# Half of a modulation's later columns computed by TensorE products instead of VectorE sums

## The chip, the core and the metric

The kernel runs on one core of one Trainium2 chip. Its engines are TensorE (PE in the rows, its weight loads PEld), VectorE (DVE), ScalarE (ACT), GpSimd (POOL) and SyncE (SP, which issues the transfers). The metric is the device time of one launch in microseconds, as the median of several runs.

## The reference, cut to what matters

Two transformer blocks of two layers each run one after the other over 512 tokens of width 1024; the first block also carries a context of 256 tokens. Each layer of the first block is steered by six vectors (shift, scale and gate, once for attention and once for the feed-forward part), which come from the condition vectors `c` and `c_ctx`:

```python
silu_c = jax.nn.silu(c)
silu_cc = jax.nn.silu(c_ctx)
for l in range(DEPTH):
    mod = silu_c @ w_ada[l] + b_ada[l]
    sh_a, sc_a, g_a, sh_f, sc_f, g_f = jnp.split(mod[:, None, :], 6, axis=-1)
    mc = jnp.split(silu_cc @ w_ada[l][:, :n_c] + b_ada[l][:n_c], n_c // d)
    hx = rmsnorm(x) * (1 + sc_a) + sh_a
    ...
    x = x + g_a * (jnp.concatenate([fx, ax, rx], axis=-1) @ w_out[l])
    x = x + g_f * swiglu(rmsnorm(x) * (1 + sc_f) + sh_f, w_gate[l], w_up[l], w_down[l])
```

So `mod` is a product of two vectors (1024 values each) with a matrix of 1024 x 6144, in single precision.

## The kernel before

Activations lie with the feature on the partition, so a vector of 1024 values is eight columns of 128. The six steering vectors of a layer are 48 columns; `mod[l][:, q, j]` is column j for the tokens (q = 0) or for the context (q = 1). Column j needs the 128 x 1024 slice `w_ada[l, j]`, one transfer of 512 KB. Columns 0 to 15 of layer 0 (shift and scale of the attention part) are made in an opening stage, `opening`, before anything else can run. Columns 16 to 39 of layer 0 are made by the generator `mod_cols` during the first mixing stage (attention, a gated recurrence called hgrn, and a Fourier mix), columns 40 to 47 and those of layer 1 during the first feed-forward stage. In the mixing stage all of them go the same way: for each of the two condition vectors one VectorE instruction (L524) multiplies the 128 x 1024 slice with the silu vector, which `sic[q]` holds on all partitions, and sums each row into one value of `mod`. In the opening some columns go another way, marked `"P"`: eight TensorE products (L1662) take a 128 x 128 block of the slice, stored in transposed order, as weights and the two silu vectors (`csil`, 128 x 2) as the moving side, and so make both values of the column in a bank of PSUM at once.

Matrix products of the layers are done in three rounds of rounded halves (`mm3`, L246 to L248): high times high, high times low, low times high. Each weight tile of 128 x 1024 is loaded, rounded by ScalarE (L231), and its rest taken by VectorE or GpSimd (L233).

The mixing stage `Mix1.rest` weaves generators: `dense` (all projections of the normed input), `hgrn(0)` and `hgrn(1)`, `fourier`, `attention` (which starts when `dense` is done) and `mod_cols`; `_weave` takes the next step of the one with the least time spent by numbers written in the code (`MCOST`, 4 units per column and vector). That fixes the program's order; a scheduler with a timing model of its own then places the instructions of each engine. Buffers come from an arena that hands out the slot which has been free the longest, and PSUM is eight banks handed out in the same way. Each engine runs its queue in order. SyncE's queue is also in order: a transfer into a slot that is not free yet holds up all transfers behind it.

Lines that the prediction's steps touch: L519 (issue of `w_ada`), L524 (the product and sum), L526 and L527 (the same on GpSimd and ScalarE, used in layer 1), L538 (adds `b_ada`), L1662 (the opening's TensorE columns), L757 (a product with a 128 x 2 moving side in `heads`), L893 and L898 (hgrn's products and their merge), L871 (the first step of an hgrn), L912 (its decay factors), L614 (transposes), L1007 (split of the queries), L588, L592 and L593 (softmax: maximum, scaling of it, exponential), L1036 (transposes of its result).

Of the kernel before, what the change touches and what calls it, by code (L numbers as in the profile page):

```python
# [12 lines left out]
AF = mybir.ActivationFunctionType  # L13
# [4 lines left out]
KD = 8  # L18
# [45 lines left out]
class _Arena:  # L64
# [32 lines left out]
    def fr(self, *bufs):  # L97
        for b in bufs:
            if isinstance(b, (list, tuple)):
                self.fr(*b)  # L100
                continue
            h = b.home
            assert (h.freed[b.o:b.o + b.u] == np.inf).all()
            h.clock += 1
            h.freed[b.o:b.o + b.u] = h.clock
# [28 lines left out]
def scaled(g, f):  # L134
    for c in g:
        yield c and c * f
# [7 lines left out]
def _body(tc, xc, cvec, w_ada, w_in, w_four, w_out, gu, dn, cols, ab_in, ab_out, gates, c_in, c_out,  # L144
          k_id, k_hs, k_lm, k_cm, k_dft, k_dftc, k_bd, k_rope, xsc, out, stop=None, dbg=None, mark=lambda n: None):
    nc = tc.nc
    V, A, G, PE, SP = nc.vector, nc.scalar, nc.gpsimd, nc.tensor, nc.sync
# [9 lines left out]
    with es:  # L157
# [8 lines left out]
        mod = [per.tile([128, 2, 48], F32, name=f"mod{i}") for i in range(2)]  # L166
        hpost = per.tile([128, 48], F32, name="hpost")
        csil = per.tile([128, 16], F32, name="csil")
# [15 lines left out]
        al, alr, fr = arena.al, rarena.al, arena.fr  # L184
# [17 lines left out]
        pf_ = banks.fr  # L202
# [311 lines left out]
        def mod_cols(l, jobs, which, sic):  # L514

            for j0, n, plus1 in jobs:
                for j in range(j0, j0 + n):
                    r = al(1024)
                    (G if MODQ else SP).dma_start(r.f, w_ada[l, j])  # L519
                    for q in which:  # L520
                        t = r if q == which[-1] else al(1024)
                        acc = mod[l][:, q, j:j + 1]
                        if j % 4 in MODV[l]:
                            V.scalar_tensor_tensor(t.f, r.f, 1.0, sic[q].f, op0=ALU.mult, op1=ALU.mult, accum_out=acc)  # L524
                        else:
                            G.tensor_tensor(t.f, r.f, sic[q].f, ALU.mult)  # L526
                            A.activation(t.f, t.f, AF.Copy, accum_out=acc)  # L527
                        if t is not r:
                            fr(t)
                    fr(r)  # L530
                    yield MCOST * len(which)
                mod_fin(l, j0, n, plus1, which)
# [84 lines left out]
        class Mix1(Phase):  # L617
# [491 lines left out]
            def rest(self, nxt):  # L1109
# [6 lines left out]
                mods = () if last else (mod_cols(0, MODS, (0, 1), self.sic),)  # L1116
                c = PACE[l]
                h0, h1, fo, at = (scaled(g, c[i]) for i, g in ((1, self.hgrn(0)), (1, self.hgrn(1)), (3, self.fourier()), (2, self.attention())))
# [659 lines left out]
OPEN = ('P', 'VV', 'P', 'P', 'P', 'VV', 'P', 'VV', 'P', 'VV', 'P', 'P', 'P', 'VV', 'P', 'VV')  # L1778
# [9 lines left out]
PRE = (3, 0, 2, 2, 3)  # L1788
ONPOOL = ('dg1', 'dh001', 'dh002', 'dh003', 'dh004', 'dh005', 'dh006', 'dh007', 'dh101', 'dh102', 'dh103', 'dh104', 'dh105', 'dh106', 'dh107', 'ka005', 'ka011', 'ka012', 'ka013', 'ka014', 'ka015', 'ka016', 'ka017', 'ka112', 'ka113', 'ka114', 'ka115', 'ka116', 'ka117', 'kk00', 'kl1', 'ma0', 'og10', 'qa001', 'qa002', 'qa003', 'qa004', 'qa005', 'qa006', 'qa007', 'qa011', 'qa012', 'qa013', 'qa015', 'qa016', 'qa101', 'qa102', 'qa103', 'qa104', 'qa105', 'qa106', 'qa107', 'qa111', 'qa112', 'qa116', 'qa117', 'qm00', 'qm11', 'r11', 'r20', 'r21', 'zd1')
MODQ = 0  # L1790
PACE = ((1.2, 1, 1, 1, 0), (1, 1.2, 0.85, 1, 0), (1, 1.5, 1))
MODV = ((0, 1, 2, 3), (2,))
ADAV = ((2, 4, 6), (0, 2, 4, 5), (0, 2, 4, 6))
POSTG = ((0, 1, 2, 3, 4, 5, 6, 7),) * 5 + ((0, 2, 4),)
MCOST = 4.0
# [10 lines left out]
def _feat(v):  # L1806

    v = np.asarray(v)
    return v.reshape(-1, 128).T
# [61 lines left out]
def _pack(inp):  # L1871
    a = {k: np.asarray(v) for k, v in inp.items()}
    r = _constants()
    xc = np.concatenate([a["ctx"][0], a["x"][0]], 0)
    r["xc"] = np.ascontiguousarray(xc.T.reshape(KD, 128, W).transpose(1, 0, 2))
    r["cvec"] = np.stack([a["c"][0], a["c_ctx"]])
    r["w_ada"] = np.ascontiguousarray(a["w_ada"].transpose(0, 2, 1).reshape(2, 48, 128, D))
    for j in range(2 * KD):
        if OPEN[j] == "P":
            r["w_ada"][0, j] = _blk(a["w_ada"][0][:, j * 128:j * 128 + 128], KD, 1).reshape(128, D)  # L1880
    r["w_in"] = np.stack([_blk(a["w_in"][l], KD, 18) for l in range(2)])
    r["w_four"] = np.ascontiguousarray(a["w_four"].reshape(2, 2, 128, 256).transpose(0, 2, 1, 3))
    r["w_out"] = np.stack([_blk(a["w_out"][l], KD, KD) for l in range(2)])
    fs = [("w_gate", "w_up", "w_down", l) for l in range(2)]
    for l in range(2):
        fs += [(f"ffn{i}_w_gate_2", f"ffn{i}_w_up_2", f"ffn{i}_w_down_2", l) for i in (1, 2)]
    r["gu"] = np.stack([np.stack([_blk(a[n][l], KD, NF) for n in (g, u)], 2) for g, u, _, l in fs])
    r["dn"] = np.stack([_blk(a[d][l], NF, KD) for _, _, d, l in fs])
    r["ab_in"] = _blk(a["ab_w_in_2"][0], KD, 20)
    r["ab_out"] = _blk(a["ab_w_out_2"][0], KD, KD)  # L1890
    ci = _blk(a["c_w_in_2"][0], KD, 24).reshape(3, KD, 128, KD, 128)
    r["c_in"] = np.ascontiguousarray(ci[[1, 2, 0]].transpose(1, 0, 2, 3, 4))
    r["c_out"] = _blk(a["c_w_out_2"][0], KD, KD)
    g = np.zeros((128, 4, 256), np.float32)
    for i, n in enumerate(("lru_gate_a_w_2", "lru_gate_x_w_2")):
        for h in range(8):
            o = h % 2 * 64
            g[o:o + 64, h // 2, i * 128 + o:i * 128 + o + 64] = a[n][0, h]
    r["gates"] = g
    two = lambda v: np.concatenate([v, v])  # L1900
    cols = np.zeros((128, NCOL), np.float32)
    vals = {
        "b_ada0": _feat(a["b_ada"][0]), "b_ada1": _feat(a["b_ada"][1]),
        "cc": _feat(r["cvec"]), "lb": _feat(a["hg_lb_logits"]), "fin": _feat(a["final_norm"]),
        "pre": _feat(a["norm_pre_2"]), "post": _feat(a["norm_post_2"]),
        "lconv": a["lru_conv_w_2"][0].reshape(4, 4, 128).transpose(2, 1, 0).reshape(128, 16),
        "lconvb": _feat(a["lru_conv_b_2"]), "lba": _feat(a["lru_gate_a_b_2"]), "lbx": _feat(a["lru_gate_x_b_2"]),
        "llam": _feat(a["lru_lambda_2"]),
        "cconv": a["c_conv_w_2"][0].reshape(3, KD, 128).transpose(2, 1, 0).reshape(128, 24),
    }  # L1910
    for l in range(2):
        vals[f"qn{l}"] = two(a["q_norm"][l])[:, None]
        vals[f"kn{l}"] = two(a["k_norm"][l])[:, None]
        vals[f"hn{l}"] = two(a["hg_norm"][l])[:, None]
    for n, (o, w) in _COLS.items():
        cols[:, o:o + w] = vals[n]
    r["cols"] = cols
    return {n: np.ascontiguousarray(r[n]) for n in _INS}
# [17 lines left out]
```

## Time and profile before

| | |
|---|---|
| median of 3 runs | 3787.3 us |
| lowest, highest | 3782.1, 3798.88 us |
| the profiled execution | 3782.26 us |
| its span | 3780.3 us |
| PE busy | 3631.1 us (96%), 19768 instructions |
| PEld busy | 3121.2 us (83%) |
| DVE busy | 1903.9 us (50%) |
| ACT busy | 1425.1 us (38%) |
| POOL busy | 557.7 us (15%) |
| mean granted clock of PE | 0.983 |

The span is the time from the first to the last instruction; 1.96 us of the execution lie outside it. Busy time of PE is modelled: products are pipelined, so that a busy PE need not be at its peak. The profile's PEclk is the granted clock: 1.00 is 2.4 GHz and 0.50 is 1.2 GHz. The stages that matter here: the opening up to about 58 us, the projections (`dense`) with hgrn(0) up to about 257 us, attention with hgrn(1) and Fourier up to about 480 us, then the output projection and the feed-forward stage.

### The profile page before, as it was taken

What the parts mean: (1) busy time and instruction counts of PE and PEld (TensorE: products, weight loads), DVE (VectorE), ACT (ScalarE), POOL (GpSimd) and SP (SyncE); (2) the same over time, 40 slices, a digit from 0 to 9 for tenths busy, and PEclk for the clock granted to TensorE, in tenths of its full rate; (3) what the DMA queues carried; (4) which work ended last, traced back from release to release, by engine and by line L of the source; (5) the groups of instructions that cost most, each with busy time, mean ns of one, the idle gap of its engine ahead of it and who ended that gap; (6) DMA issues with size and microseconds to landing.
All of it is one profiled execution on the core that took longest, in us unless ns stands there. A gap on an engine that the chain in (4) does not pass through costs nothing. (4 is left out here: it accounts for less than half of the span.)

```text
span 3780.3 us, 48445 instructions
## 1 busy us (share of the span) xinstructions
PE 3631.1 (96%) x19768; PEld 3121.2 (83%) x19768; DVE 1903.9 (50%) x2833; ACT 1425.1 (38%) x2410; POOL 557.7 (15%) x499
## 2 busy tenths in 40 slices
PE   7998899999999989999999999999999999999998
PEld 7876698888887869888988886788888888888887
DVE  6677655533344775333533367562345234645234
ACT  4235643342243474323432335442234233334222
POOL 1331012550013400000100031110011001111001
PEclk9998999999999999999999999999999999999999
DMA  6322114453212122423132221133222322223322
GB/s 210 93 73 85 44 44 137 150 188 99 76 40 71 40 80 76 134 73 110 59 106 89 93 77 62 51 109 104 86 82 96 106 86 88 91 89 104 107 71 76
DMA packets 95823, 345.12 MB, mean 91 GB/s; under 512 B 10864, under 2 KB 14064, under 8 KB 95600
## 3 DMA queue, kind: packets, MB, share of 16 engines
q1 hardware_dynamic: 95024, 341.50, 28.0%
q8 instruction: 155, 2.54, 0.3%
q14 instruction: 68, 0.56, 0.0%
q10 hardware_dynamic: 576, 0.52, 0.0%
HBM read 334.64 MB, written 4.19 MB: 90 GB/s over the span
## 5 line engine op out<-in xcount | busy, mean ns | idle before, releaser
L246 PE MATMUL psum<-rarena,room 128*128 128x512 f32 (+1 forms) x3041 | 1071.4, 354 | 9.1 <-ACT room L231 3.9
L247 PE MATMUL psum<-rarena,room 128*128 128x512 f32 (+1 forms) x3041 | 1071.5, 353 | 1.8 <-DVE rarena L1193 1.1
L248 PE MATMUL psum<-rarena,room 128*128 128x512 f32 (+1 forms) x2955 | 1049.9, 356 | 0.7 <-DVE room L233 0.7
L248 PE MATMUL psum<-rarena 128*128 128x512 f32 (+1 forms) x2118 | 737.9, 349 | 7.8 <-DVE rarena L233 7.7
L246 PE MATMUL psum<-rarena 128*128 128x512 f32 (+1 forms) x2032 | 722.6, 357 | 8.5 <-ACT rarena L213 3.3
L247 PE MATMUL psum<-rarena 128*128 128x512 f32 (+1 forms) x2032 | 720.0, 354 | 2.0 <-DVE rarena L1193 1.8
L246 PEld LDWEIGHTS psum<-rarena,room 128*128 128x128 f32 x3041 | 575.8, 190 | 88.4 <-ACT room L231 5.2
L247 PEld LDWEIGHTS psum<-rarena,room 128*128 128x128 f32 x3041 | 576.6, 190 | 80.8 <-DVE rarena L1193 1.9
L248 PEld LDWEIGHTS psum<-rarena,room 128*128 128x128 f32 x2955 | 559.6, 190 | 80.6 <-DVE room L233 1.4
L233 DVE TENSOR_TENSOR room<-arena,room 128x1024 fp32r<-128x1024 f32 (+2 forms) x252 | 329.8, 1314 | 553.6 <-PE psum L247 238.4
L231 ACT ACTIVATE room<-arena 128x1024 fp32r<-128x1024 f32 (+2 forms) x290 | 319.8, 1110 | 647.6 <-PE psum L248 205.3
L299 POOL TENSOR_TENSOR arena<-arena 128x256 f32<-128x256 f32 x170 | 140.1, 832 | 2264.4 <-ACT arena L297 2218.4
L248 PEld LDWEIGHTS psum<-rarena 128*128 128x128 f32 x2118 | 402.5, 190 | 59.9 <-DVE rarena L233 9.8
L246 PEld LDWEIGHTS psum<-rarena 128*128 128x128 f32 x2032 | 386.2, 190 | 62.6 <-ACT rarena L213 3.8
L247 PEld LDWEIGHTS psum<-rarena 128*128 128x128 f32 x2032 | 386.4, 190 | 54.4 <-DVE rarena L1193 2.2
L231 ACT ACTIVATE rarena<-arena 128x1024 fp32r<-128x1024 f32 (+2 forms) x141 | 158.1, 1123 | 360.2 <-PE psum L248 107.6
L233 DVE TENSOR_TENSOR rarena<-arena,rarena 128x1024 fp32r<-128x1024 f32 (+2 forms) x104 | 137.6, 1324 | 254.0 <-PE psum L247 121.8
L213 ACT ACTIVATE rarena<-arena 128x256 fp32r<-128x256 f32 (+2 forms) x253 | 130.2, 532 | 239.3 <-DVE arena L436 209.0
L214 DVE TENSOR_TENSOR rarena<-arena,rarena 128x256 fp32r<-128x256 f32 (+2 forms) x246 | 139.7, 582 | 121.2 <-ACT rarena L213 121.1
L436 DVE TENSOR_TENSOR arena<-arena,psum 128x512 f32<-128x512 f32 (+1 forms) x170 | 100.4, 598 | 166.7 <-PE psum L248 149.0
L297 ACT ACTIVATE arena<-arena 128x256 f32<-128x256 f32 (+1 forms) x274 | 105.8, 412 | 191.6 <-DVE arena L1262 82.2
L526 POOL TENSOR_TENSOR arena<-arena 128x1024 f32<-128x1024 f32 x48 | 129.1, 2701 | 222.1 <-DMA arena<-w_ada 108.4
(366 smaller groups left out, 4186.2 us busy)
## 6 DMA issues: line engine op xcount, KB each, us to landing
arena<-gu SPq DMA_DIRECT2D x264, 512.0 KB, 3.7
arena<-dn SPq DMA_DIRECT2D x80, 704.0 KB, 4.1
arena<-w_ada SPq DMA_DIRECT2D x57, 512.0 KB, 3.8
room<-w_ada SPq DMA_DIRECT2D x39, 512.0 KB, 4.4
room<-w_in SPq DMA_DIRECT2D x31, 512.0 KB, 3.7
arena<-c_in SPq DMA_DIRECT2D x24, 512.0 KB, 3.6
arena<-dn SPq DMA_DIRECT2D x16, 448.0 KB, 3.5
room<-ab_in SPq DMA_DIRECT2D x13, 512.0 KB, 3.6
```

The source lines that it names most:

```text
L213: A.activation(h, src, AF.Copy)
L214: eng.tensor_tensor(lo, src, h.bitcast(F32), ALU.subtract)
L231: A.activation(h.r, r.f, AF.Copy)
L233: (G if wlo[1] < wlo[0] else V).tensor_tensor(lo.r, r.f, h.f, ALU.subtract)
L246: PE.matmul(ps, h[:, s], ah, start=k == 0, stop=False)
L247: PE.matmul(ps, h[:, s], al_, start=False, stop=False)
L248: PE.matmul(ps, lo[:, s], ah, start=False, stop=k == nk - 1)
L297: A.activation(sq.f, src, AF.Square)
L299: (V if self.fast else G).tensor_tensor(self.parts[0].f, self.parts[0].f, sq.f, ALU.add)
L436: V.tensor_tensor(s.f, s.f, pu, ALU.mult)
L526: G.tensor_tensor(t.f, r.f, sic[q].f, ALU.mult)
```

## The change

Of layer 0's columns 16 to 39, the twelve even ones up to 38 leave VectorE. Each becomes eight TensorE products with the slice's blocks as weights and the two silu vectors as the moving side, into a PSUM bank of its own, and one ScalarE copy of the 128 x 2 result into `mod`. The host stores those twelve slices in blocks, as it did for the opening's columns. The number of transfers and their size stay.

```diff
                 for j in range(j0, j0 + n):
                     r = al(1024)
                     (G if MODQ else SP).dma_start(r.f, w_ada[l, j])
+                    if l == 0 and j in MODP:
+                        p = ps(2)
+                        for k in range(KD):
+                            PE.matmul(p.f, r.f[:, k * 128:k * 128 + 128], csil.rearrange("p (q k) -> p k q", q=2)[:, k], start=k == 0, stop=k == KD - 1)
+                        A.activation(mod[l][:, :, j], p.f, AF.Copy)
+                        pf_(p)
+                        fr(r)
+                        yield MCOST * len(which)
+                        continue
                     for q in which:
 ...
+MODP = (16, 18, 20, 22, 24, 26, 28, 30, 32, 34, 36, 38)
 ...
-    for j in range(2 * KD):
-        if OPEN[j] == "P":
+    for j in range(48):
+        if j in MODP or j < 2 * KD and OPEN[j] == "P":
             r["w_ada"][0, j] = _blk(a["w_ada"][0][:, j * 128:j * 128 + 128], KD, 1).reshape(128, D)
```

Nine lines are inserted at L520, so a line L of before from there on is L + 9 in the changed kernel (L524 becomes L533, L246 stays). The new products are L523, the new copies L524. The scheduler moves other instructions too. Three places show it.

On PE, where a projection's 512-token part ends and the next block's 256-token part begins (246 to 248 are the three rounds of a projection's product), before:

```order
L247 MATMUL psum<-rarena 128x512
L248 MATMUL psum<-rarena 128x512
L246 MATMUL psum<-rarena 128x256
L247 MATMUL psum<-rarena 128x256
L248 MATMUL psum<-rarena 128x256
```

and now, at the same products, on PE:

```order
L247 MATMUL psum<-rarena 128x512
L248 MATMUL psum<-rarena 128x512
L523 MATMUL psum<-csil,room 128x2 x8
L246 MATMUL psum<-rarena 128x256
L247 MATMUL psum<-rarena 128x256
L248 MATMUL psum<-rarena 128x256
```

A column's eight products stand in the middle of the stream of projections. Nine of the twelve columns stand before the end of `dense`, three behind it.

On DVE, at the end of `dense`, where hgrn(1)'s decay factors (L912) are made ahead of its first step (L871), before:

```order
L912 TENSOR_TENSOR room<-arena 128x768
L881 TENSOR_TENSOR room<-arena 128x768
L912 TENSOR_TENSOR room<-room 128x384
L912 TENSOR_TENSOR room<-room 128x192
L912 TENSOR_TENSOR room<-room 128x96
```

and now (the same lines are L921 and L890), on DVE:

```order
L921 TENSOR_TENSOR room<-arena 128x768
L533 SCALAR_TENSOR_TENSOR room,mod_66<-room,arena 128x1024
L890 TENSOR_TENSOR room<-arena 128x768
L921 TENSOR_TENSOR room<-room 128x384
L533 SCALAR_TENSOR_TENSOR room,mod_66<-room,arena 128x1024
L921 TENSOR_TENSOR room<-room 128x192
L921 TENSOR_TENSOR room<-room 128x96
```

One remaining VectorE column now stands inside this run of instructions; the last factors, the queries' split and the two multiplications of L871 (L880 now) follow it in both.

On DVE, in the first softmax tiles of attention (L588 is the maximum, L898 hgrn's merge, L214 a split, L599 the sum of an output's halves), before:

```order
L898 COPY_PREDICATED room<-lm,psum 128x384 x3
L524 SCALAR_TENSOR_TENSOR room,mod_66<-room,arena 128x1024
L214 TENSOR_TENSOR rarena<-psum,rarena 128x512
L524 SCALAR_TENSOR_TENSOR room,mod_66<-room,arena 128x1024
L588 TENSOR_REDUCE room<-psum 128x1
L214 TENSOR_TENSOR rarena<-psum,rarena 128x512
L588 TENSOR_REDUCE room<-psum 128x1
L898 COPY_PREDICATED room<-lm,psum 128x384 x3
L599 TENSOR_TENSOR arena<-psum,room 64x512
L588 TENSOR_REDUCE room<-psum 128x1
L524 SCALAR_TENSOR_TENSOR room,mod_66<-room,arena 128x1024
```

and now, on DVE:

```order
L907 COPY_PREDICATED room<-lm,psum 128x384 x4
L214 TENSOR_TENSOR rarena<-psum,rarena 128x512
L597 TENSOR_REDUCE room<-psum 128x1
L214 TENSOR_TENSOR rarena<-psum,rarena 128x512
L597 TENSOR_REDUCE room<-psum 128x1
L907 COPY_PREDICATED room<-lm,psum 128x384 x3
L608 TENSOR_TENSOR arena<-psum,room 64x512
L597 TENSOR_REDUCE room<-psum 128x1
```

The column's products and sums no longer stand between the splits and the maxima.

## Rows read from the trace of the kernel before

**Rows 1.** Busy time by stretch: start:end length, busy us (instructions), PEclk, DMA share, GB/s.

```profile
58.00:250.00 192.00, 181.01 (x1148) 157.73 (x1149) 125.43 (x236) 61.16 (x123) 62.75 (x52) 0.96 0.31 99
250.00:450.00 200.00, 167.30 (x934) 133.84 (x934) 151.53 (x282) 127.72 (x273) 39.26 (x33) 0.89 0.19 60
...
900.00:1000.00 100.00, 100.00 (x585) 88.91 (x584) 28.17 (x37) 21.10 (x30) 0.00 (x0) 1.00 0.19 61
```

**Rows 2.** PE's waits of 58 to 250 us: for whom, us, times, longest.

```profile
PE psum L893 <- POOL room L881: 2.4, 1, 2.4
PE psum L893 <- POOL arena L871: 2.3, 1, 2.3
PE psum L246 <- DVE arena L898: 2.0, 1, 2.0
...
PE psum L757 <- ACT arena L753: 1.7, 1, 1.7
```

**Rows 3.** PE's waits of 250 to 350 and of 350 to 450 us.

```profile
PE psum L893 <- DVE arena L871: 4.8, 1, 4.8
PE psum L1036 <- ACT room L593: 3.0, 4, 1.7
PE psum L1036 <- DVE arena L608: 1.4, 1, 1.4
...
PE psum L1036 <- ACT room L593: 14.3, 12, 3.8
```

**Rows 4.** L524: instructions (ns min/median/max), waits in 58 to 400 us, one wait.

```profile
L524 DVE SCALAR_TENSOR_TENSOR room<-room,arena x46: 1197/1225/3414, 58.1 to 367.8; 128x1024 f32<-128x1024 f32 x46
L524 DVE DVE_READ_ACCUMULATOR room<-room,arena x46: 75/81/85, 59.2 to 368.9; 128x1 f32 x46
...
  DMA room<-w_ada: 11.8, 6
...
71.78 1.23 DVE L524 SCALAR_TENSOR_TENSOR room<-room,arena 128x1024 f32<-128x1024 f32 x1 [5.01 <-DMA room<-w_ada]
```

**Rows 5.** L524 alone by stretch: DVE's busy us, instructions (two per product), PEclk, DMA.

```profile
250.00:300.00 50.00, 5.25 (x8) 0.93 0.12 36
300.00:350.00 50.00, 9.26 (x12) 0.83 0.23 71
```

**Rows 6.** The opening's TensorE columns in order of time: start, length, count.

```profile
24.72 14.93 PE L1662 MATMUL psum<-csil,room 128*128 128x2 f32 x70
...
44.15 3.63 PE L1662 MATMUL psum<-csil,room 128*128 128x2 f32 x32
47.64 6.61 PE L1729 MATMUL psum<-rarena 128*128 128x256 f32 x36
54.08 4.87 PE L1662 MATMUL psum<-csil,room 128*128 128x2 f32 x32
```

**Rows 7.** Busy time by stretch around these, as in rows 1; PEclk is third from the end.

```profile
46.00:48.00 2.00, 2.00 (x18) 2.00 (x19) 1.96 (x4) 0.67 (x1) 1.27 (x1) 1.00 0.29 55
...
56.00:58.00 2.00, 2.00 (x13) 2.00 (x12) 1.05 (x3) 0.81 (x1) 0.00 (x0) 0.55 0.93 258
...
62.00:64.00 2.00, 2.00 (x10) 1.68 (x10) 0.97 (x2) 2.00 (x3) 0.00 (x0) 0.74 0.67 244
```

**Rows 8.** Groups of PE in 58 to 480 us: L757, products with a 128x2 moving side.

```profile
L757 PE MATMUL psum<-hs,room 128*128 128x2 f32 x36 | 4.6, 243 | 1.0 <-ACT room L753 0.9
```

**Rows 9.** PE in order of time around 90 us.

```profile
89.67 0.66 PE L614 MATMUL psum<-ident,room 128*128 128x128 f32 x4
92.66 3.67 PE L893 MATMUL psum<-arena,room 64*128 64x128 f32 x24 [2.34 <-POOL arena L871]
```

**Rows 10.** DVE in order of time at the end of `dense`.

```profile
249.35 0.96 DVE L912 TENSOR_TENSOR room<-arena 128x768 f32<-128x768 f32 x1 [8.16 <-ACT arena L670]
...
261.54 3.43 DVE L871 TENSOR_TENSOR arena<-arena 128x768 f32<-128x768 f32 x2
```

**Rows 11.** A small ScalarE instruction, from the groups of the whole span.

```profile
L592 ACT ACTIVATE room<-room,arena 128x1 f32<-128x1 f32 x49 | 14.0, 289 | 22.0 <-DVE room L588 21.8
```

## The prediction

> **What bounds the kernel now.** The page gives PE 96% of the span, so a change that adds PE work has to be read stage by stage. First the busy time by stretch [rows 1]. From 58 to 250 us, while the projections run, PE is busy 181.0 of 192 us and DVE 125.4. From 250 to 450 us, in attention, PE is busy 167.3 of 200 and DVE 151.5: there PE stands still for 32.7 us and runs at a mean granted clock of 0.89. After that the feed-forward stage has PE at 100% [rows 1]. The columns that the change touches all lie in the first two stretches: 48 DVE products of L524 between 58 and 368 us [rows 4]; ten of them lie between 250 and 350 us (20 instructions, two per product) [rows 5].
>
> Then who makes PE wait. From 58 to 250 us the waits are few: two for POOL (4.7 us together), one of 2.0 us for DVE's merge L898, one of 1.7 us for ACT [rows 2], and nothing else over 1.1 us. No PE product waits for a DVE column there. Behind 250 us PE waits 4.8 us for DVE's L871, 1.4 us for DVE's L608, and 3.0 and 14.3 us for ACT's exponentials [rows 3], which come behind DVE's maxima. So **PE bounds the projections, and a chain PE, DVE, ACT, PE bounds attention**. DVE had room in the first stretch and less in the second.
>
> **The change part by part.** It removes 24 DVE products. Each costs 1.225 us, and the sum's read-out of 0.08 us overlaps but little [rows 4]; with the gap the next one starts 1.3 us later, so DVE gets 24 x 1.3 = 31 us less. Transfers stay as many and as large; each slot is now released by PE for half the columns.
>
> It adds 96 TensorE products in single precision. The opening has such columns: a run of 32 in [rows 6] is two of them, so a column is 16 products of the hardware (two for each one of the program). Their pace is there too: 32 take 47.64 - 44.15 = 3.49 us, 0.109 us each, at a granted clock of 1.00 [rows 7]. A column is then 16 x 0.109 = 1.75 us. Two other rows bound it from above: L757, also with a moving side of 128x2, takes 4.6 / 36 = 0.128 us, 2.05 us a column [rows 8]; the opening's first long run takes 14.93 / 70 = 0.213 us, 3.4 us a column [rows 6]. I take 1.75, because the new columns stand between dense products, as those 32 did.
>
> Where they stand: I took each column's neighbours in the new order of PE and looked up the same products, counted by line, in the trace of before. They lie at 89, 110, 136, 164, 167, 202, 223, 232 and 248 us, and then at 281, 314 and 328 us.
> - Nine in the projections. The first has three of its eight products before the four transposes of L614 and five behind them, and there PE waited 2.34 us for POOL [rows 9], so that the five are hidden: 0.4 of a column remains. The other eight stand in the stream. 8.4 x 1.75 = **+14.7 us**; 17.2 at L757's pace, 28.6 at the slow one.
> - Three in attention, among products where PE waits 17.3 us for exponentials [rows 3]. I hide half: 3 x 1.75 / 2 = **+2.6 us**, between 0 (all in waits) and 10.2 (none, slow pace).
> - A PE product must now wait for the slice to land, and PE's whole queue behind it. DVE waited 11.8 us in six waits for 24 columns; 5.0 of it was one wait at 71.8 us, ahead of any new column [rows 4]. That leaves 6.8, half of it 3.4 for twelve columns. The columns on PE are ordered later relative to their transfers at the start; I take half of that, **+1.7 us**, between 0 and 3.4.
> - The granted clock. After the 32 products of 44 us it stayed at 1.00, but while the next 32 of 54 us ran it fell to 0.50: the slice from 56 to 58 us has a mean of 0.55, and that from 62 to 64 us 0.74, so it was low from about 56.2 to 63.0 us [rows 6, 7]. 6.8 us at half the clock cost 3.4 us where PE bounds. A column alone is half such a run. I take **+1.0 us**, a third of one such stretch; between 0 and three of them, 10.2.
> - Twelve ACT copies of 128x2: 0.289 us each by the nearest small instruction [rows 11], 3.5 us together. ACT is busy 61 of 192 us in the projections [rows 1], so nothing. If that cover were gone (three of them lie in attention), 0.9 us. Each holds one of eight PSUM banks a little longer; no row prices that, and with 1 of 8 banks I take nothing.
>
> What DVE's relief gives back. In the projections only the waits that DVE ended can shorten: 2.0 us, and half of it is **-1.0**. In attention ten products become four by the new order, so about 8 us of DVE work leave the stretch from 262 to 330 us. The waits that it can touch are 3.0 + 1.4 us, and a part of the 14.3 [rows 3]: **-4.0**, between 0 and -8. Against that stands one column which the new order puts among the decay factors L912 ahead of L871. DVE ran from 249.35 us without a pause into L871 at 261.54 us [rows 10], and PE waited for just that [rows 3]. Two products are 2.6 us; half, **+1.3**, because ACT, for which the first factor waited 8.16 us [rows 10], may set the start anyway.
>
> Sum: 14.7 + 2.6 + 1.7 + 1.0 - 1.0 - 4.0 + 1.3 = **+16.3 us**. The profiled execution took 3782.26 us, so 3798.6 us in its terms. The median of the runs lies 5.0 us above it; 3787.3 + 16 = **3803 us**. Nothing of PE's order differs before 88 us, so the opening gives and takes nothing. Behind 480 us PE is full; the later stages' orders differ in places (slots are handed out in another sequence), which I leave at zero. The added biases (L538) now wait for ACT too, but the first gate is needed behind 450 us.
>
> 0.5%, about what a measurement of this kernel can tell from no change, is 19 us. So the forecast is **a little slower, within 0.5%**.
>
> **The rivals.**
> 1. *The clock falls in the projections* (slower). The new products are thin, as those at 54 us. Several stand next to others of hgrn that are thin too: at 110, 136, 164 and 167 us. If each of these four places lowers the clock as at 56 us, the cost is 4 x 3.4 = 13.6 us in place of 1.0: +29 us, 3816 us. For it: PE did not wait ahead of 56 us either [rows 6]. Against it: the run of 44 us was twice as long as a column and left the clock at 1.00 [rows 7]. It decides from two such stretches on (+22 us).
> 2. *DVE's relief frees attention* (faster). PE's idle time from 250 to 450 us is 32.7 us, and at a clock of 0.89 it spends some 44 us at half speed (2 x 0.11 x 200), which may cost up to 22 us [rows 1]. If half of both go, that is -27 us in place of -2.7 for the two terms there, with the three late columns hidden: about -11 us, 3776 us. For it: DVE is 76% busy there. Against it: the largest waits name ACT, and behind 330 us the new order has as many columns as the old one.
> 3. *The products fit beside the weight loads* (no change). PEld is busy 157.7 of 192 us in the projections [rows 1]; 34.3 us are free, and the nine columns need 9 x 1.75 = 15.7 us of loads. Then the first term is nearly 0, the sum +2, 3789 us. For it: busy PE is a modelled figure. Against it: where PE is full, PEld is at 88.9% [rows 1], which in 192 us is 170.7, so 13.0 us are free, and the waits at the head of PE's queue [rows 2] make up most of those. The Trainium skill, Perfetto Trace Analysis, Identifying the Most-Contended Engine, calls the share of busy weight loads the better measure of TensorE's headroom, and busy matmul time a bad one; by that rule this rival would hold, while the row at 88.9% puts its ceiling below 100%.
>
> That the change does not do what it says can be set aside: in the new order 24 of L524's products are gone and 96 on PE are there.
>
> **How the numbers follow.** Forecast: 0.42, spread from 3795 to 3811, of which 0.12 lies above 3806 (slower by over 0.5%). Rival 1: 0.24, all slower. Rival 2: 0.18, of which 0.11 reach below 3768, since that takes 34 of the 55 us that could be had at most, and 0.07 stay within. Rival 3: 0.16, within. So faster 0.11, same 0.30 + 0.07 + 0.16 = 0.53, slower 0.12 + 0.24 = 0.36. The range of 8 in 10 goes from 3780 (leaving out most of rival 2) to 3818 (leaving out the upper part of rival 1); the forecast's own is 3795 to 3811.
>
> **What would show each step.** In the profile of the changed kernel: the new products' start to start (0.109 us, or over 0.2); the end of the projections, when L871's successor starts (about 13 us later than 261.5); the granted clock from 100 to 250 us (0.96 to 1.00 if rival 1 is wrong); PE's waits for `w_ada` (a few us); PE's waits for exponentials and for hgrn(1)'s first step, which is rival 2. If the projections end at the same time as before, the first term is wrong and rival 3 right. If they end 13 us later and the total is unchanged or lower, the step on attention was too small.

## The result and the profile after

The changed kernel takes 3839.6 us (median of 4 runs, 3835.57 to 3841.8), the kernel before 3791.75 us in the same comparison (4 runs, 3782.1 to 3798.88). The ratio is 1.0125, interval 1.011 to 1.014: **47.9 us slower**, where 16 were forecast, and above the range, which ended at 3818. The profiled execution of the changed kernel took 3840.08 us and has a span of 3838.1 us. The profiled execution of before lies 9 us below its median in this comparison, at a granted clock of 0.983, where the executions of before on record beside the experiments have 0.974 to 0.982; so distances between those two traces come out about 10 us too large in sum.

The head of the page of the changed kernel: PE has 192 instructions and 43.6 us more than in the table of before, DVE 43.7 us less.

```profile
span 3838.1 us, 48819 instructions
PE 3674.7 (96%) x19960; PEld 3158.9 (82%) x19960; DVE 1860.2 (48%) x2785; ACT 1424.4 (37%) x2421; POOL 547.9 (14%) x499
```

Busy time by stretch in the changed kernel, columns as in [rows 1], whose first two rows the first two here answer. The third stretch is layer 0's feed-forward stage, the fourth layer 1's mixing stage:

```profile
58.00:250.00 192.00, 187.65 (x1228) 166.18 (x1228) 96.13 (x194) 58.51 (x123) 63.00 (x52) 0.94 0.30 96
250.00:450.00 200.00, 171.18 (x974) 136.87 (x973) 129.35 (x252) 114.09 (x250) 35.17 (x32) 0.91 0.16 50
580.00:900.00 320.00, 296.80 (x1649) 259.37 (x1647) 134.64 (x171) 109.17 (x176) 109.36 (x44) 0.97 0.42 139
1100.00:1450.00 350.00, 321.16 (x1903) 272.73 (x1902) 212.57 (x412) 164.59 (x343) 95.94 (x106) 0.95 0.17 55
```

The last two stretches in the kernel before:

```profile
580.00:900.00 320.00, 312.72 (x1781) 275.48 (x1780) 149.95 (x181) 115.93 (x188) 129.15 (x48) 0.99 0.49 154
1100.00:1450.00 350.00, 320.14 (x1864) 268.93 (x1864) 225.49 (x397) 180.15 (x368) 91.26 (x99) 0.97 0.21 65
```

The projections are as forecast: PE fuller, DVE emptier by 29.3 us, the clock 0.94 after 0.96. But in the feed-forward stage, which the change doesn't touch, PE is busy for 15.9 us less of the 320, and DMA moves 139 GB/s where it moved 154. Shifted to about the same products (607 to 942 us in the changed kernel), PE stands still for 24.9 us there, where it was 7.3.

**Where the time went** is read by matching PE's products in both traces, each with the same line and count, and taking the median difference of their start times. Besides the changed kernel the table has four of the experiments below (their names are explained there); the stretches are by the time of the kernel that is subtracted, in us.

| stretch | after - before | e5 - before | e6 - before | e3 - e1 | e4 - e1 |
|---|---|---|---|---|---|
| 250 to 275, end of the projections | 13.4 | 14.6 | 0 to 1 | 19.4 | -1.2 |
| about 475 to 550, end of attention | 23.1 | 19.7 | 0 to 1 | 28.8 | -7.4 |
| 600 to 650, feed-forward | 27 to 29 | 24.6 | 9.5 | 32.4 | -5.5 |
| 850 to 1100 | 42.3 to 43.2 | 24.6 | 22.8 | 32.4 | -5.5 |
| from 1400 on | 58.6 | 27.7 | 37 to 39.6 | 30 | -5.5 |

So 13 us were lost in the projections, 10 in attention, 20 in layer 0's feed-forward stage and 15 in layer 1's mixing stage; from 1400 us to the end nothing moves. The first two are in the forecast's stretches. The last two are what it left at zero. How far one pair of traces can be trusted is seen in e1, e6, e7 and e8 below: up to about 540 us they have before's instructions in before's order, and yet at 475 us they are 3.8, 0.9, 4.9 and 1.0 us later than before. A distance in the table is good to some 5 us.

### The profile page after: what moved, and what is told of

It is laid out like the page before. It is cut to its first block, busy times and chain, and to the rows that moved or that the text cites. A ratio compares the mean times of both kernels' runs of the same rounds, so it can differ in the third digit from the quotient of the medians.

```text
span 3838.1 us, 48819 instructions
## 1 busy us (share of the span) xinstructions
PE 3674.7 (96%) x19960; PEld 3158.9 (82%) x19960; DVE 1860.2 (48%) x2785; ACT 1424.4 (37%) x2421; POOL 547.9 (14%) x499
## 5 line engine op out<-in xcount | busy, mean ns | idle before, releaser
L246 PE MATMUL psum<-rarena,room 128*128 128x512 f32 (+1 forms) x3041 | 1072.9, 354 | 17.6 <-ACT room L231 12.3
L246 PE MATMUL psum<-rarena 128*128 128x512 f32 (+1 forms) x2032 | 725.0, 358 | 16.1 <-ACT rarena L231 10.4
L246 PEld LDWEIGHTS psum<-rarena,room 128*128 128x128 f32 x3041 | 577.2, 190 | 97.6 <-ACT room L231 13.7
L231 ACT ACTIVATE room<-arena 128x1024 fp32r<-128x1024 f32 (+2 forms) x290 | 320.1, 1110 | 662.0 <-PE psum L248 221.5
L246 PEld LDWEIGHTS psum<-rarena 128*128 128x128 f32 x2032 | 388.6, 191 | 70.6 <-ACT rarena L231 11.6
L231 ACT ACTIVATE rarena<-arena 128x1024 fp32r<-128x1024 f32 (+2 forms) x138 | 154.8, 1124 | 376.2 <-PE psum L248 95.6
L213 ACT ACTIVATE rarena<-arena 128x512 fp32r<-128x512 f32 (+2 forms) x252 | 129.7, 530 | 254.2 <-DVE arena L436 227.8
L214 DVE TENSOR_TENSOR rarena<-arena,rarena 128x512 fp32r<-128x512 f32 (+1 forms) x245 | 140.2, 586 | 95.7 <-ACT rarena L213 95.5
L535 POOL TENSOR_TENSOR arena<-arena 128x1024 f32<-128x1024 f32 x48 | 119.5, 2498 | 267.6 <-DMA arena<-w_ada 152.8
```

The costliest lines, as they stand in the source:

```text
L213: A.activation(h, src, AF.Copy)
L214: eng.tensor_tensor(lo, src, h.bitcast(F32), ALU.subtract)
L231: A.activation(h.r, r.f, AF.Copy)
L246: PE.matmul(ps, h[:, s], ah, start=k == 0, stop=False)
```

## The experiments

**The theories.** A: the change has two separate prices, its own work in the first mixing stage (about what the sum says), and another order of the later stages, since slots of the on-chip arena and PSUM banks are handed out least recently freed first, the changed kernel frees them in another sequence, and the scheduler then orders what follows differently. B: the later loss comes from the change's work itself (DMA, the clock, products that DVE's remaining columns wait for). C, which is rival 2 turned round: the relief of DVE is real and large, and the products cost still more than thought. The measurements are compared by medians, since one profile may be 10 us off; a difference is given in medians, its interval by the ratios.

**1. The history of the slots wiped at the start of the feed-forward stage**, in both kernels, so that the stages behind it hand out slots by address alike:

```diff
             if p is f0:
+                for _h in (arena, rarena, banks):
+                    _h.freed[_h.freed < np.inf] = 0
```

In the kernel before (e1_reset_before), expected:

> The kernel before, with the history of the free slots (both arenas and the PSUM banks) wiped when the first feed-forward stage starts, so that what the mixing stage did no longer decides which slot is handed out there. No work is added or taken away. The order theory (the changed kernel lost some 35 us behind the mixing stage only because slots were handed out in another sequence and the queues were ordered anew) expects a time within 15 us of the kernel before, 3775 to 3805, since any sequence is as good as another up to such a spread. The work theory (the new products themselves disturb the later stages) expects the same here, and differs in the next kernel.

In the changed kernel (e2_reset_after), expected:

> The changed kernel with the same wiping of the slots' history at the start of the first feed-forward stage. The order theory expects what the mixing stage alone costs: 15 to 30 us above the run before it in this set (e1_reset_before), and from 600 us on the same distance to its end. The work theory expects 45 to 60 us above it, with the distance growing between 600 and 900 us and between 1100 and 1450 us as in the changed kernel.

Measured: e1 3810.64 us, beside 3789.57 of before, ratio 1.0053 (1.0036 to 1.007); e2 3834.07 us, ratio 1.0113 (1.0093 to 1.0133). Wiping the history, which changes no work, cost before 21 us, more than the 15 that were expected at most, and left the changed kernel about where it was. Between the two the change is worth 23.4 us and not 47.9. By start times their distance is 21 us at the end of attention and stays within 22 to 29 us behind 550 us, so with like histories the later stages add little.

**2. The products alone, and the relief alone**, both on e1. For the products, 96 of them on the same slices into a column of layer 1 that is overwritten later, while DVE keeps all its columns:

```diff
+                    if l == 0 and 16 <= j < 40 and j % 2 == 0:
+                        p = ps(2)
+                        for k in range(KD):
+                            PE.matmul(p.f, r.f[:, k * 128:k * 128 + 128], csil.rearrange("p (q k) -> p k q", q=2)[:, k], start=k == 0, stop=k == KD - 1)
+                        A.activation(mod[1][:, :, j], p.f, AF.Copy)
+                        pf_(p)
```

> The kernel before with wiped history, and beside the VectorE products, which all stay, the twelve even columns are also run through TensorE (8 products and one ScalarE copy each) into columns that nobody reads; the slices keep the VectorE layout, so those products are of no use and only their time counts. If TensorE bounds the projections and VectorE's relief is worth little, this costs as much as the full change: 15 to 30 us above e1_reset_before. If the relief is worth its 4 to 5 us, this costs 5 us more than e2_reset_after does. If the products fit beside weight loads, 0 to 5 us.

For the relief, the twelve columns leave DVE and no product takes their place, so that they aren't computed:

```diff
+                    if l == 0 and 16 <= j < 40 and j % 2 == 0:
+                        A.activation(mod[l][:, :, j], r.f[:, 0:2], AF.Copy)
+                        fr(r)
+                        yield MCOST * len(which)
+                        continue
```

> The kernel before with wiped history, in which the twelve even columns from 16 to 38 of layer 0 are not computed at all: one small ScalarE copy from the landed slice stands in for both VectorE products of each (that part of the computation is left out). 31 us of VectorE work are gone and nothing is added on TensorE. The theory that VectorE bounds nothing in the projections expects 0 to 5 us below e1_reset_before. The theory that VectorE's relief frees attention expects 10 to 25 us below it.

Measured: e3 3843.65 us, ratio 1.0137 (1.0116 to 1.0157), 33.0 us over e1, a little above the 15 to 30 expected; e4 3809.94 us, ratio 1.0047 (1.0028 to 1.0066), 0.7 us under e1. Taking 24 products of 1.2 us off DVE brings nothing that the total shows: the executions of e1 and e4 spread over 9 and 15 us, so a gain of some 5 us could hide in them, but not the 10 to 25 of theory C, which falls. The products cost more than their own 20.5 us (twelve times 1.71, below) when DVE isn't relieved as well; e3 - e2 is 9.6 us, but the intervals of the two overlap.

What became of the relief is seen in attention, by stretches cut at the same products (the last three end some 4 us of work sooner, in which PE is full). The rows are, in turn, before, the changed kernel, e1, e3 and e4:

```profile
262.00:475.00 213.00, 179.45 (x997) 144.45 (x998) 154.65 (x296) 134.02 (x291) 32.44 (x24) 0.90 0.20 62
```

```profile
275.00:496.00 221.00, 186.19 (x1036) 149.26 (x1037) 141.10 (x281) 131.56 (x292) 32.38 (x23) 0.89 0.19 60
```

```profile
262.00:475.00 213.00, 180.39 (x978) 144.37 (x979) 151.26 (x292) 130.68 (x286) 33.21 (x23) 0.86 0.20 62
```

```profile
281.00:503.00 222.00, 187.36 (x1020) 149.38 (x1021) 154.63 (x298) 134.72 (x295) 33.23 (x26) 0.88 0.19 60
```

```profile
261.00:468.00 207.00, 174.54 (x995) 138.81 (x994) 142.36 (x283) 132.34 (x294) 32.23 (x27) 0.92 0.21 64
```

PE's idle time (length less busy) is 33.6, 34.8, 32.6, 34.6 and 32.5 us: within 2.3 us of each other in all five, with 9 to 14 us less of DVE or not. With the columns gone e4 is 6 us shorter than e1, but at a granted clock of 0.92 after 0.86, not by less idle time. What PE waits for changes, though. Its waits in that stretch, the largest and the like of them, in before and then in the changed kernel:

```profile
PE psum L1036 <- ACT room L593: 19.9, 18, 3.8
PE psum L893 <- DVE arena L871: 4.8, 1, 4.8
...
PE psum L1036 <- ACT arena L593: 0.8, 1, 0.8
```

```profile
PE psum L1045 <- ACT room L602: 9.0, 13, 1.4
PE psum L1050 <- DVE rarena L214: 3.9, 4, 2.2
PE psum L1045 <- ACT arena L602: 3.4, 3, 2.3
PE psum L286 <- DVE arena L284: 2.3, 1, 2.3
...
PE psum L902 <- DVE arena L880: 1.7, 1, 1.7
```

The waits of L1036 (L1045 now) for exponentials fell from 20.7 to 12.4 us and that for hgrn(1)'s first step from 4.8 to 1.7; waits for splits (L214) and others came in their place.

**3. The histories exchanged.** The numbers that say when each slot and bank was last freed were read out where the feed-forward stage begins. The same slots are free there in both kernels; all 96 free pieces of the arena (24 slots of 1024 values) and 8 of 8 banks have other times, while those of the second arena, `rarena`, are the same. Each kernel was given the numbers of the other (`HIST`, a table not shown here):

```diff
             if p is f0:
+                for _h, runs in zip((arena, rarena, banks), HIST):
+                    then = np.concatenate([np.full(n, v, float) for n, v in runs])
+                    assert ((then < 0) == np.isinf(_h.freed)).all()
+                    _h.freed[then >= 0] = then[then >= 0]
+                    _h.clock = max(_h.clock, int(then.max()))
 ...
```

The changed kernel with the history of before (e5_after_old_history), expected:

> The changed kernel, in which the free slots of both arenas and of PSUM get, at the start of the first feed-forward stage, the very history that they have there in the kernel before (written into the code as numbers; the same slots are free in both). The order theory expects the feed-forward stage's and layer 1's queues to fall back to nearly the old order, and the time to what the mixing stage costs alone: 3790 + 23 = 3813, between 3805 and 3822. The work theory expects the changed kernel's 3835 to 3842 again.

The kernel before with the history of the changed one (e6_before_new_history), expected:

> The kernel before, without any TensorE column, with the history of the free slots that the changed kernel has at that point. No work is added or moved in the mixing stage. The order theory expects the whole loss behind that stage and nothing ahead of it: 3790 + 25 to 35 = 3815 to 3825. The work theory expects 3790.

Measured: e5 3809.5 us, beside 3792.29 of before, ratio 1.0048 (1.0033 to 1.0063), +17.2 us (12.5 to 23.9); e6 3820.09 us, ratio 1.0074 (1.0054 to 1.0094), **+27.8 us with not one instruction's work changed**. The four kernels make a square, in us over the median of before beside them:

| | history of before | history of the changed kernel |
|---|---|---|
| work of before | 0 | +27.8 |
| work of the changed kernel | +17.2 | +47.9 |

17.2 + 27.8 = 45.0 of 47.9: the two prices add. Theory A holds, and B, by which e5 would have stayed near +48 and e6 near 0, falls. In the table of start times e5 keeps its 24.6 us (24.2 to 24.8) from 600 to 1150 us, and e6 keeps step with before until 550 us and loses from there.

How e6 loses in the feed-forward stage: busy time by stretch of e6, for the two later stages, to be set against the rows of before above:

```profile
580.00:900.00 320.00, 299.87 (x1673) 262.49 (x1672) 132.51 (x164) 110.51 (x178) 111.55 (x45) 0.97 0.44 142
1100.00:1450.00 350.00, 318.72 (x1845) 270.73 (x1844) 218.22 (x420) 169.87 (x355) 91.49 (x100) 0.93 0.18 56
```

and of e5, which has these later stages as before has them in the first, and nearly so in the second:

```profile
580.00:900.00 320.00, 310.05 (x1767) 272.98 (x1766) 154.25 (x188) 117.08 (x189) 125.42 (x47) 0.99 0.49 158
1100.00:1450.00 350.00, 321.99 (x1904) 273.09 (x1903) 220.90 (x403) 178.37 (x372) 92.41 (x101) 0.95 0.18 58
```

PE's longest waits from 540 to 900 us (for whom: us, times, longest), before and then e6:

```profile
PE psum L246 <- ACT room L231: 3.9, 3, 3.1
PE psum L246 <- ACT rarena L213: 3.3, 1, 3.3
```

```profile
PE psum L246 <- ACT rarena L231: 8.3, 2, 5.5
PE psum L246 <- ACT room L231: 6.0, 3, 3.4
PE psum L261 <- ACT rarena L213: 5.6, 1, 5.6
PE psum L246 <- ACT rarena L213: 5.2, 2, 4.2
```

All of PE's waits there come to 11.9 us in before and 26.9 in e6. The division holds for every kernel here: 9.7 to 17.2 us in the four with before's history at this place (before, e5, and e9 and e10 below), 19.8 to 28.1 in the other eight.

L231 rounds a weight tile as it has landed. Its own wait is for the transfer, as ACT and PE of e6 show, in order of time:

```profile
603.30 1.06 ACT L231 ACTIVATE room<-arena 128x1024 fp32r<-128x1024 f32 x1 [5.48 <-DMA arena<-gu]
```

```profile
604.41 0.58 PE L246 MATMUL psum<-rarena,room 128*128 128x256 f32 x1 [3.42 <-ACT room L231]
```

And the transfer is late in SP's queue, which issues the stage's `w_ada` slices (L519; columns 40 to 47 of layer 0, then those of layer 1) and the feed-forward weights `gu` (L230) one behind the other, in an order that differs. SP in order of time, before and then e6:

```profile
565.40 10.04 SPq L230 DMA_DIRECT2D arena<-gu  x5
580.08 24.22 SPq L519 DMA_DIRECT2D arena<-w_ada  x5
```

```profile
586.69 10.22 SPq L519 DMA_DIRECT2D arena<-w_ada  x4
598.57 22.67 SPq L230 DMA_DIRECT2D arena<-gu  x4
```

Before issues five weight tiles ahead of five slices; e6 puts four slices ahead, three of which wait for a slot that an earlier column still holds, and the weights queued behind them wait too. The longest such case is in e7 of the next experiment, where one slot was turned and nothing else: SP, then ACT and PE, in order of time.

```profile
802.39 23.31 SPq L519 DMA_DIRECT2D arena<-w_ada  x8
...
847.05 9.33 SPq L230 DMA_DIRECT2D arena<-gu  x3
```

```profile
853.71 1.06 ACT L231 ACTIVATE room<-arena 128x1024 fp32r<-128x1024 f32 x1 [5.15 <-DMA arena<-gu]
```

```profile
854.82 0.58 PE L246 MATMUL psum<-rarena,room 128*128 128x256 f32 x1 [16.92 <-ACT room L231]
```

No `gu` is issued from 802 to 847 us, and PE stands still for 16.9 us; the longest wait of before in this stage is 3.3. How long SP waits in sum tells less: for slots that columns still hold (L524 and L527), L519 waited 93.0 us from 540 to 920 us in before and 142.1 in e6, but 83.1, 95.2 and 90.5 in e1, e7 and e8, which lose time there as well. What the rows show is the place in the queue.

The changed kernel has a like row for the longest wait of PE there, in order of time:

```profile
622.36 0.58 PE L246 MATMUL psum<-rarena,room 128*128 128x256 f32 x1 [5.92 <-ACT room L231]
```

**4. Is it the changed kernel's history, or any other than before's?** Two small turns of the kernel before: one slot taken and given back at that place (e7_one_slot_turned), and two slots and a bank (e8_two_slots_a_bank).

```diff
             if p is f0:
+                fr(al(1024))
```

> The kernel before, in which one 128 x 1024 slot is taken and given back when the first feed-forward stage starts; no instruction comes of it, but the slots are handed out from the next one on. If the sequence of before is a lucky or picked one among many, this costs 10 to 25 us, as wiping did (3800 to 3815). If the sequence usually matters little and the two other sequences were unlucky, it stays within 8 us of 3790.

```diff
             if p is f0:
+                pf_(ps())
+                fr(al(1024), al(1024))
```

> The kernel before with two slots and one PSUM bank taken and given back at the same point, again with no instruction. The expectations are those of e7_one_slot_turned: 3800 to 3815 if before's sequence is a lucky one, within 8 us of 3790 if the sequence usually matters little. With it there are four sequences of the slots beside before's to compare.

Measured: e7 3812.42 us, ratio 1.0054 (1.0034 to 1.0073), +20.1; e8 3811.58 us, ratio 1.0053 (1.0037 to 1.0069), +19.3. So all four other sequences that were tried, e1, e6, e7 and e8, cost 19 to 28 us. The changed kernel's 27.8 is the most, but its interval overlaps those of the others; that of before is the best of the five.

Part of this cost comes with a lower granted clock. The 33 executions of before beside the experiments take 3781 to 3788 us at a mean granted clock of 0.982, 3792 to 3798 at 0.977 and 3802.5 at 0.974: some 2.4 us for each 0.001. Kernels with before's history have 0.978 to 0.979 in the mean of their executions, those with another 0.973 to 0.977. Set beside before at a like clock, along a straight line through those 33, e1 and e7 are still 10 and 11 us slower, e8 14 and e6 20, and e5 17 (an estimate). So up to half of what another sequence costs goes with the clock, and the rest doesn't; what lowers the clock isn't shown.

**5. The change's own part split**, on e5 (the history of before): the nine early columns alone (e9_nine_early), the three late ones alone (e10_three_late).

```diff
-MODP = (16, 18, 20, 22, 24, 26, 28, 30, 32, 34, 36, 38)
+MODP = (16, 18, 20, 22, 24, 26, 28, 30, 32)
```

> As e5_after_old_history (the change with the old history of the slots in the feed-forward stage), but only the nine columns 16 to 32, whose products stand among the projections, go to TensorE; 34, 36 and 38 stay on VectorE. If every column costs its 1.71 us of TensorE where the projections run and nothing is won in attention, this is 12 to 18 us above the kernel before (3802 to 3808), with all of it there by 275 us. If the three columns in attention carry a good part of e5's 17 us, it is under 10 us above it. The mixing stage's distance at 275 us is expected at 13 to 16 us in both.

```diff
-MODP = (16, 18, 20, 22, 24, 26, 28, 30, 32, 34, 36, 38)
+MODP = (34, 36, 38)
```

> As e9_nine_early with the other three: only 34, 36 and 38 go to TensorE, 16 to 32 stay on VectorE, old history of the slots. If the products hide in TensorE's waits in attention and take VectorE work out of it, this is within 5 us of the kernel before (3785 to 3797), and 0 to 5 us later at 475 us. If they cost as e5 and e2 had it from 275 to 475 us, it is 5 to 8 us later there.

Measured: e9 3808.52 us, ratio 1.0042 (1.003 to 1.0055), +16.6, within the 12 to 18 expected; e10 3798.96 us, ratio 1.0013 (1.0 to 1.0026), +7.0 in medians and +5 by the ratio. Together 23.6, or 21 by the ratios, beside the 17.2 of all twelve; with intervals of 11 to 21, 0 to 10 and 12.5 to 23.9 us that is in keeping with a plain sum. By start times, set against before as in the table, e9 has the projections' end 14.7 us later, as with all twelve, and e10, with no product there, 2.3. At the end of attention e9 is 26.4 us later, though no product of the change stands in attention, and e10 13.0 to 13.5, where 8 were expected at most. Both are far above what the medians leave in the end; e9's trace had a granted clock of 0.86 in attention (276 to 500 us), where before had 0.90. So the totals can be split, and attention's share of them can't. No kernel tried beats the one before.

## Why the prediction was wrong, step by step

**The products' pace and the nine columns: right.** One column in the stream of the projections, PE of the changed kernel in order of time (start, length, ...):

```profile
241.46 0.39 PE L248 MATMUL psum<-rarena 128*128 128x512 f32 x1
241.68 1.84 PE L523 MATMUL psum<-csil,room 128*128 128x2 f32 x16
243.38 0.37 PE L246 MATMUL psum<-rarena 128*128 128x256 f32 x1
```

243.38 - 241.68 = 1.70 us for 16 products, 0.106 each, where 0.109 was taken from [rows 6]; the other whole columns of the projections take 1.70 or 1.71. 1.75 us a column was a good price. The projections end 13.4 us later by the table and hgrn(1)'s first step starts 12.0 us later than in [rows 10], where about 13 were forecast. DVE of the changed kernel in order of time:

```profile
264.35 4.00 DVE L533 SCALAR_TENSOR_TENSOR room<-room,arena 128x1024 f32<-128x1024 f32 x1
...
273.55 1.83 DVE L880 TENSOR_TENSOR arena<-arena 128x768 f32<-128x768 f32 x2
```

**Waits for the slices: overrated.** 1.7 us were taken, one wait of 0.8 us came, in the changed kernel's group of the products (busy us, mean ns, then the idle time before them):

```profile
L523 PE MATMUL psum<-csil,room 128*128 128x2 f32 x192 | 23.0, 248 | 1.2 <-DMA room<-w_ada 0.8 <-DVE arena L608 0.5
```

**The clock: one half-speed stretch more in the trace, where a third of one was taken; that the columns made it isn't shown.** Busy time by stretch from 160 us, the changed kernel:

```profile
160.00:173.00 13.00, 12.69 (x95) 11.20 (x95) 5.97 (x14) 2.31 (x5) 0.30 (x1) 1.00 0.83 204
173.00:183.00 10.00, 7.28 (x34) 5.77 (x34) 3.94 (x8) 6.65 (x14) 4.69 (x2) 0.50 0.42 156
```

and the same 10 us in the kernel before:

```profile
173.00:183.00 10.00, 10.00 (x71) 9.32 (x70) 6.89 (x15) 6.00 (x13) 4.46 (x3) 1.00 0.80 263
```

It begins behind the two columns at 164.6 and 169.3 us, in the changed kernel, in e2, e5 and e9 alike, and isn't there in before and e1; PE stood still for 2.7 of the 10 us as well. Three other low stretches are there in both kernels. But e4, which has none of the columns, has one as long, behind 10.4 us of which PE stood still for 3.2:

```profile
160.00:170.40 10.40, 7.19 (x58) 5.91 (x58) 2.09 (x6) 1.86 (x3) 1.30 (x1) 1.00 1.03 231
170.40:180.60 10.20, 7.46 (x21) 6.01 (x22) 6.43 (x17) 5.47 (x12) 3.41 (x2) 0.50 0.26 92
```

and e3, which has all of them, has no such stretch until 182 us. So rival 1's mechanism isn't shown even in this one place; if it is there, it cost 5 us at most. The opening can't carry it either, as the prediction read it from [rows 6] and [rows 7]: right behind the 32 products of 44 us the clock stayed up in before, but fell in e6, with the same instructions in the same order. Before and then e6:

```profile
47.30:54.00 6.70, 6.70 (x41) 5.90 (x41) 5.85 (x10) 3.00 (x4) 0.00 (x0) 1.00 0.46 157
47.30:54.00 6.70, 6.70 (x25) 5.93 (x26) 5.85 (x13) 2.52 (x4) 0.00 (x0) 0.50 0.50 157
```

One trace shows where the clock fell in one execution, and no more. That the end of the projections moved by no more than 13 to 15 us has its reason in PE's idle time of 58 to 250 us: 192 - 181.0 = 11.0 us in [rows 1], 192 - 187.65 = 4.4 us in the changed kernel. In e6, e7 and e8, which have before's instructions there, it is 6.9 to 8.2 us. So the columns filled some 2.5 to 6.6 us of waits, where the forecast took only 1.0 out of them: 9 x 1.71 = 15.4, plus up to 5, less these, is 9 to 18 us.

**Attention: mis-sized.** 2.6 for the products less 4.0 for the relief, plus 1.3, made -0.1. Measured, the stretch is 6 us (e5) to 8 us (after) longer, as far as one trace tells: e1, with before's instructions there, is 4 us longer by start times. I hid half of the late columns in waits, but PE's idle time didn't shrink, so all three count in full (5.1 us). I let the relief shorten the waits for exponentials, which it did (20.7 to 12.4), while others filled the gap; e4, with the relief alone, is 6 us shorter here in its trace, at a higher clock, and 0.7 in the medians, so whether the -4.0 came at all isn't settled. The price of a later L871 didn't come: PE waited 1.7 us for it, where it had waited 4.8. Rival 2's sum has a slip beside this: to be faster by 0.5% it needs 35 of its 55 us, not 34.

**The sum for the change itself: right in size, and partly by luck.** 16.3 forecast, 17.2 measured in e5 (interval 12.5 to 23.9), with two of its terms off against each other: more waits were filled in the projections than it took, and attention cost more. With the other two pairs of like histories it comes to 20.1 (after less e6) and 23.4 (e2 less e1).

**The step that failed** is the sentence "the later stages' orders differ in places (slots are handed out in another sequence), which I leave at zero". It was a term of +28 us (e6), nearly twice the rest of the sum. Its reason was that PE is full behind 480 us, and that was read from one row, of 900 to 1000 us [rows 1]. The rows of before above don't bear it out: PE stood still for 7.3 us from 580 to 900 us and for 29.9 from 1100 to 1450. And where PE is nearly full, an order of SP's queue that puts `w_ada` ahead of `gu` makes a new wait, as e6 and e7 show (PE's waits from 540 to 900 us: 11.9 us, then 26.9 and 23.2). The new order was there to be read ahead of the result; its price wasn't.

**The rivals.** Rival 1 (the clock) has at most one place of four and isn't what made the difference: e5 has the same stretch and lies at +17. Rival 2 (DVE's relief frees attention, 27 us) fails by e4: 0.7 us in sum. Rival 3 (the products fit beside the weight loads) fails by e5, e9 and e3: the nine columns moved the end of the projections by 14.6, 14.7 and 19.4 us, although PEld had 34 us free in [rows 1].

**What stays open.** In the feed-forward stage the chain from the slot to SP, the transfer, L231 and PE is seen in the trace, but no run took one single slot's wait away. In layer 1's mixing stage the loss was located (1100 to 1450 us, a clock of 0.93 in e6 after 0.97) and not traced to a slot or a bank. By start times e1, e7 and e8 lose half or more of theirs there too, but e9, with before's history, has a clock of 0.93 in that stretch as well and loses 9 us; so some of what the table shows there may belong to the profiled execution of before, which lies 9 us under its median, at the highest clock of its executions. History and order can't be told apart by these runs, because the scheduler makes a new order for each history. Whether a sequence better than that of before exists wasn't tried beyond the four.

## What to carry to other kernels

Where slots are handed out by when they were last freed and a scheduler orders by a model, an edit can be two edits: its own work, and a new order of all that follows. Run the edit once with the old history, and the old work once with the new history, before judging either; here every other history cost, 19 to 28 us in four of four. And where PE is full, price thin products by their start-to-start time in full, whatever the share of the weight loads says.

## What the runs showed of the hardware

A turn of one slot in an otherwise unchanged kernel costs 20 of 3790 us (e7), about as much as the twelve columns' own work (17.2). And one of DVE's 1024-wide sums took 4.00 us, in the row at 264.35 us, where most take 1.225 [rows 4]; GpSimd ran a multiplication of 128x768 beside it for 2.9 of them. The row, of POOL in the changed kernel:

```profile
264.10 3.16 POOL L916 TENSOR_TENSOR arena<-arena 128x768 f32<-128x768 f32 x1 [22.73 <-DVE room L890]
```

No run took one of them away, but the twelve traces hold 840 of these sums: none of the 583 without a GpSimd instruction beside it took over 1.23 us, and each of the 134 that took over 1.3 us had one beside it, as had 123 that didn't.
